# A Hymba-style decoder block: two plain tiles of the up-projection instead of three, with the activations' differences made beside their sums

## The chip, the cores and the metric
The kernel runs on one core of one Trainium2 chip. The metric is the device time of one launch in microseconds (us); lower is better. Engines are called TensorE, VectorE, ScalarE, GpSimd and SP (the queue that issues the transfers); in the profile they are PE (PEld is its weight load), DVE, ACT, POOL and SP.

## The reference, cut to what matters
One decoder block on 1024 tokens and 16 learned meta tokens, model width 1024. Two groups of attention heads read one projection; their outputs go through one output projection and are added to the residual. Then, and only this part is touched by the change:

```python
def _conv_ffn(xn, w_up, conv_w, conv_b, w_down):
    L = xn.shape[1]
    h = xn @ w_up
    hp = jnp.pad(h, ((0, 0), (CONV_WIDTH - 1, 0), (0, 0)))
    hc = conv_b + sum(conv_w[k] * hp[:, k:k + L] for k in range(CONV_WIDTH))
    gate, up = jnp.split(hc, 2, axis=-1)
    return (jax.nn.silu(gate) * up) @ w_down
```

`xn` is the normalised residual, 1024 wide, `w_up` is 1024 x 5632 and `w_down` 2816 x 1024, all in float32. A final norm follows.

## The kernel before, in words
**Precision.** Each float32 product is made of three matmuls on rounded numbers: every operand is split into a high part (ScalarE copies it to the matmul type) and a low part (the rest, by a subtraction), and high x high, high x low and low x high are summed in PSUM.

**The up-projection.** `w_up` is cut into 22 pairs of tiles of 128 columns (a gate tile and an up tile), called ff. The first `PLAIN` (3) pairs are multiplied plainly: a plain chunk (`plain_chunk`, L919) takes one pair and 256 tokens (plus 2 for the convolution), has 8 x 3 matmuls of 258 columns for the gate and as many for the up tile (48), then convolution, SiLU, product and a store to `gated`. `plain_chunk(..., h, s)` means half h of the sequence and quarter s in that half, so a pair has four chunks. The other 19 pairs go through the loop at L1105, which multiplies a 2 x 2 block form with seven products instead of eight (Strassen's scheme in Winograd's form): gate and up tile, the two halves of the model width and the two halves of the sequence are the blocks. A pass of it has 7 x 24 = 168 matmuls of 258 columns.

**What the loop needs.** Its activations are four blocks of the transposed input and four combinations: `s1`, `s2`, `s4` (made by `block_sums`, L970) and `s3` (made by `block_difference`, L984, written over a block of the input that only plain chunks of the second half still read). Both work on the rows of the normalised input, stored to DRAM earlier as `y_rows`, one block of 128 rows at a time (t = 4, 3, 2, 1, and t = 0 with two rows): `block_sums` loads the rows of both halves into tiles with the tags "ta" and "tb" (one buffer each), makes three combinations on VectorE (L978, L979, L980) in tiles `sa` (tag "wh") and `sb` (tag "wl"), and has TensorE transpose them (L180, four transposes of 128 x 128 for a half row); ScalarE and VectorE split the result (L183, L184). `block_difference` loads half rows into `rd` (tag "wl", L988, L989), subtracts in place (L990) and does the same. The tags "wh" and "wl" have two buffers each in the pool `pw`. The second plain pair's up tile has its parts in one buffer of each (`plain_weights`, L944, `last and i`), until its last chunk.

The loop's weights are prepared by `load_up` (L1035): gate and up tile are loaded raw, and four GpSimd subtractions (L1041 to L1044) make the combinations in tiles "ta" and "tb", the same buffers as the rows. `split_w` (L903) then splits each in 1.05 us of ScalarE (L907) and 2.4 us of GpSimd (L908). The order of a pass is: first product with the raw gate tile, second and third with `tb`, and so on.

**Order.** The kernel's text is an order of priority: a scheduler at compile time simulates the engines and fixes each engine's order of instructions; each engine then runs its instructions strictly in that order, waiting at semaphores. SP, too, issues transfers in its fixed order. A tile takes a free buffer of its tag when there is one, and waits for a release otherwise.

Around the change, the first two pairs' chunks of the second half stand before (L952 to L957). Then come the eight chunks, five sums and five differences of L1006 to L1024, and the loop.

Of the kernel before, what the change touches and what calls it, by code (L numbers as in the profile page):

```python
# [13 lines left out]
ALU = mybir.AluOpType  # L14
# [21 lines left out]

HALF = SEQ // 2
SUB = HALF // 2
PLAIN = 3
N_ROWS = 4  # L40
N_PAIRS = (NF - N_ROWS) // 2
G_PAIRS = 3
# [36 lines left out]
def q_span(t):  # L79

    return (0, 2) if t == 0 else (2 + P * (t - 1), P)
# [15 lines left out]
def hybrid_block(ctx: ExitStack, tc: tile.TileContext, x, meta, g_attn, w_in, lq1, lk1, lq2, lk2,  # L97
                 g_diff, g_sb, w_out, g_ffn, w_up, conv_w, conv_b, w_down, g_final, out):
    nc = tc.nc
# [6 lines left out]
    def bank(tag):  # L106
        return psum.tile([P, 512], F32, tag=tag, name=f"ps_{tag}", bufs=2)
# [39 lines left out]
    def rstd(pool, ss, n, tag):  # L147

        w = pool.tile([P, 4], F32, tag=tag, name=tag, bufs=4)
        l, y, m, u = (w[:n, i : i + 1] for i in range(4))  # L150
        nc.scalar.activation(l, ss, AF.Ln, bias=eps[:n], scale=1.0 / D)
        nc.scalar.activation(y, l, AF.Exp, scale=-0.5)
        nc.vector.tensor_scalar(m, ss, 1.0 / D, EPS, op0=ALU.mult, op1=ALU.add)
        nc.vector.tensor_scalar(u, m, y, y, op0=ALU.mult, op1=ALU.mult)
        nc.vector.tensor_scalar(u, u, -0.5, 1.5, op0=ALU.mult, op1=ALU.add)
        nc.vector.tensor_scalar(m, u, y, None, op0=ALU.mult)
        return m
# [17 lines left out]
    def transpose_half(src, n, places, tag):  # L175

        ps = bank(tag)
        v = ps.rearrange("p (a b) -> p a b", b=P)
        for j in range(4):
            nc.tensor.transpose(v[:, j, :n], src[:n, j * P : (j + 1) * P], ident[:n, :n])  # L180
        for hi, lo, c0, r0 in places:
            w = n - r0
            nc.scalar.copy(hi[:, :, c0 : c0 + w], v[:, :, r0:n])  # L183
            nc.vector.tensor_tensor(lo[:, :, c0 : c0 + w], v[:, :, r0:n], f(hi)[:, :, c0 : c0 + w], op=ALU.subtract)  # L184
# [269 lines left out]
    sums = {}  # L454
# [228 lines left out]
    def load_raw(src):  # L683
        raw = pw.tile([P, D], F32, tag="raw", name="raw", bufs=2)
        nc.sync.dma_start(raw, src)
        return raw
# [216 lines left out]
    def split_w(pool, tags, src, bufs):  # L903
        hi = pool.tile([P, D], F32R, tag=tags[0], name=tags[0], bufs=bufs)
        lo = pool.tile([P, D], F32R, tag=tags[1], name=tags[1], bufs=bufs)
        w = src.shape[-1]
        nc.scalar.copy(hi[:, :w], src)  # L907
        nc.gpsimd.tensor_tensor(lo[:, :w], src, f(hi)[:, :w], op=ALU.subtract)  # L908
        return hi, lo

    def conv(c, src, fc):

        n = c.shape[-1]
        taps = [src[:, j : j + n] if len(src.shape) == 2 else src[:, :, j : j + n] for j in range(3)]
        nc.scalar.activation(c, taps[2], AF.Identity, bias=cb[:, fc : fc + 1], scale=cw[:, fc, 2:3])
        for j in (1, 0):
            nc.vector.scalar_tensor_tensor(c, taps[j], cw[:, fc, j : j + 1], c, op0=ALU.mult, op1=ALU.add)

    def plain_chunk(ff, wts, h, s):  # L919
        cs = []  # L920
        for fc, (hi, lo), tag, ctag, bufs in ((ff, wts[0], "s", "o", 4), (NF + ff, wts[1], "av", "mc", 2)):
            ps = bank(tag)
            c0 = SUB * s
            for kt in range(KT):
                ks = slice(kt * P, (kt + 1) * P)
                for i, (a, b) in enumerate(((hi, yh[h]), (hi, yl[h]), (lo, yh[h]))):
                    nc.tensor.matmul(ps[:, : SUB + 2], a[:, ks], b[:, kt, c0 : c0 + SUB + 2],  # L927
                                     start=(kt == 0 and i == 0), stop=(kt == KT - 1 and i == 2))
            c = pn.tile([P, 342], F32, tag=ctag, name="c", bufs=bufs)[:, :SUB]
            conv(c, ps[:, : SUB + 2], fc)  # L930
            cs.append(c)
        cg, cu = cs
        nc.scalar.activation(cg, cg, AF.Silu)
        nc.vector.tensor_tensor(cg, cg, cu, op=ALU.mult)
        at = HALF * h + SUB * s
        nc.sync.dma_start(gated[ff, :, at : at + SUB], cg)
# [7 lines left out]
    def plain_weights(ff, last):  # L944
        ws = []
        for i in range(2):
            raw = load_raw(w_up[NF * i + ff])
            pool, tags, bufs = (pw, ("wh", "wl"), 2) if last and i else (pd, ("dh", "dl"), 3)
            ws.append(split_w(pool, tags, raw, bufs))
        return ff, ws  # L950
# [17 lines left out]
    HD = D // 2  # L968

    def block_sums(t):  # L970

        n, c = (P, q_span(t)[0]) if t else (2, 0)
        r0 = load_rows_of_y(y_rows[t, :n, :], n, "ta")
        r1 = load_rows_of_y(y_rows[t + NT // 2, P - n :, :], n, "tb")
        sa = pw.tile([P, D], F32, tag="wh", name="sa", bufs=2)[:n]
        sb = pw.tile([P, D], F32, tag="wl", name="sb", bufs=2)[:n]
        lo, hi = slice(0, HD), slice(HD, D)
        nc.vector.tensor_tensor(sa[:, lo], r1[:, lo], r1[:, hi], op=ALU.add)  # L978
        nc.vector.tensor_tensor(sa[:, hi], sa[:, lo], r0[:, lo], op=ALU.subtract)  # L979
        nc.vector.tensor_tensor(sb[:, hi], r0[:, hi], sa[:, hi], op=ALU.subtract)  # L980
        for (dst, src) in ((s1, sa[:, lo]), (s2, sa[:, hi]), (s4, sb[:, hi])):
            transpose_half(src, n, [(dst[0], dst[1], c, 0)], "tr")

    def block_difference(t):  # L984

        n, c = (P, q_span(t)[0]) if t else (2, 0)
        r = pw.tile([P, D], F32, tag="wl", name="rd", bufs=2)[:n]
        nc.sync.dma_start(r[:, :HD], y_rows[t, :n, :HD])  # L988
        nc.sync.dma_start(r[:, HD:], y_rows[t + NT // 2, P - n :, :HD])  # L989
        nc.vector.tensor_tensor(r[:, :HD], r[:, :HD], r[:, HD:], op=ALU.subtract)  # L990
        transpose_half(r[:, :HD], n, [(s3[0], s3[1], c, 0)], "tr")

    def load_rows_of_y(src, n, tag):
        rows = ps_.tile([P, D], F32, tag=tag, name="rows")[:n]
        nc.sync.dma_start(rows, src)
        return rows

    def sums(*ts_):
        for t in ts_:
            block_sums(t)  # L1000

    def differences(*ts_):
        for t in ts_:
            block_difference(t)

    first, second = plain  # L1006
    plain_chunk(*first, 0, 1)
    sums(4)
    plain_chunk(*first, 0, 0)
    sums(3)  # L1010
    third = plain_weights(2, False)
    plain_chunk(*third, 1, 1)
    sums(2)
    plain_chunk(*third, 1, 0)
    sums(1)
    plain_chunk(*second, 0, 1)
    sums(0)
    differences(4)
    plain_chunk(*second, 0, 0)
    differences(3)  # L1020
    plain_chunk(*third, 0, 1)
    differences(2, 1)
    plain_chunk(*third, 0, 0)
    differences(0)  # L1024
    banks.close()


# [18 lines left out]

    entries = [(ff, i) for ff in range(PLAIN, NF) for i in range(4)]
    ready = {}
# [55 lines left out]
    rest = sums_of = before = None  # L1104
    for ff in range(PLAIN, NF):  # L1105
        k = 4 * (ff - PLAIN)
        pool, tag, bufs = (pw, "wh", 2) if ff % 3 else (ps_, "cg", 1)
# [102 lines left out]
    for group in groups:  # L1210
        chains = {}
        n = len(group)
        for tag, begin, rows, cs in CHAINS:
# [3 lines left out]
            for t, j in order:  # L1217
                ps = chains[tag][t]
                hi, lo = taken[k + j]
# [12 lines left out]
    for t in range(1, NT + 1):  # L1232
# [11 lines left out]
        r = rstd(pn, ss, P, "rf")  # L1244
# [44 lines left out]
```

## Time and profile before

| what | value |
|---|---|
| median of 3 runs | 1430.29 us (1428.49 to 1432.56) |
| the profiled execution's own time | 1427.61 us |
| its span in the trace | 1425.9 us |
| granted clock of TensorE, mean | 0.985 |
| TensorE busy | 1347.5 us, 95% of the span |
| VectorE, ScalarE, GpSimd busy | 967.8, 714.9, 749.2 us |

The median is of whole runs on the device; the span is what the profiler recorded of one of them. A busy time is the union of an engine's instructions. A line such as L927 is a line of the kernel printed above. In a timeline, a row gives start, duration, engine, line, operation, what is written and read, and in brackets how long the engine had been idle and what released it.

### The profile page before, as it was taken

What the parts mean: (1) busy time and instruction counts of PE and PEld (TensorE: products, weight loads), DVE (VectorE), ACT (ScalarE), POOL (GpSimd) and SP (SyncE); (2) the same over time, 40 slices, a digit from 0 to 9 for tenths busy, and PEclk for the clock granted to TensorE, in tenths of its full rate; (3) what the DMA queues carried; (4) which work ended last, traced back from release to release, by engine and by line L of the source; (5) the groups of instructions that cost most, each with busy time, mean ns of one, the idle gap of its engine ahead of it and who ended that gap; (6) DMA issues with size and microseconds to landing.
All of it is one profiled execution on the core that took longest, in us unless ns stands there. A gap on an engine that the chain in (4) does not pass through costs nothing.

```text
span 1425.9 us, 24695 instructions
## 1 busy us (share of the span) xinstructions
PE 1347.5 (95%) x9000; PEld 1251.1 (88%) x9000; DVE 967.8 (68%) x1816; ACT 714.9 (50%) x1406; POOL 749.2 (53%) x769
## 2 busy tenths in 40 slices
PE   5999989999998998899999899999999996999997
PEld 5989989998987887678899899999999995888886
DVE  7377867778676787875877546555555565977755
ACT  6355655666575666542444344444454444534322
POOL 5145444235666676852103367766776573966620
PEclk9999999999999999999999999999999998999999
DMA  5154454221211127335633222323223325966502
GB/s 215 52 184 153 151 162 144 60 68 38 60 43 40 46 59 224 84 73 140 169 122 129 78 82 92 110 97 104 77 94 97 111 91 202 325 203 191 177 15 104
DMA packets 93569, 166.35 MB, mean 117 GB/s; under 512 B 11628, under 2 KB 46060, under 8 KB 93448
## 3 DMA queue, kind: packets, MB, share of 16 engines
q1 hardware_dynamic: 93448, 164.78, 37.0%
q8 instruction: 71, 1.16, 0.4%
q14 instruction: 50, 0.41, 0.1%
HBM read 111.49 MB, written 44.85 MB: 110 GB/s over the span
## 4 chain that ended last, share of the span: by engine, by line
PE 66%; DVE 9%; issue 4%; ACT 3%; POOL 2%; DMA 1%; SPq 0%; DVEq 0%; POOLq 0%; ACTq 0%
PE x L1063 27%; PE ps_x L1221 7%; PE ps_mm L297 7%; PE ps_y L1221 5%; PE ps_mm L745 5%; DVE s L501 3%; PE ps_av L588 2%; PE ps_tr L559 2%; PE ps_s L927 2%; PE ps_av L927 2%; PE ps_x L1239 2%; PE ps_y L1239 2%; PE ps_s L444 1%; PE ps_s L445 1%; PE ps_tr L180 1%
## 5 line engine op out<-in xcount | busy, mean ns | idle before, releaser
L297 PE MATMUL ps_mm<-xT_hi,wh 128*128 128x342 f32 (+7 forms) x552 | 182.6, 331 | 4.7 <-DVE qz L307 3.2
L297 PE MATMUL ps_mm<-xT_lo,wh 128*128 128x342 f32 (+7 forms) x552 | 180.1, 327 | 0.2 <-DVE xT_lo L184 0.2
L297 PE MATMUL ps_mm<-xT_hi,wl 128*128 128x342 f32 (+7 forms) x552 | 179.2, 326 | 0.0
L588 PE MATMUL ps_av<-aT,v 128*128 128x256 f32 (+3 forms) x608 | 130.8, 306 | 4.7 <-POOL aT L566 4.1
L908 POOL TENSOR_TENSOR dl<-raw,dh 128x1024 fp32r<-128x1024 f32 (+1 forms) x43 | 82.8, 1926 | 95.3 <-ACT dh L907 95.3
L1063 PE MATMUL x<-yh,dl 128*128 128x258 f32 x608 | 124.2, 286 | 0.0
L1063 PE MATMUL x<-yh,dh 128*128 128x258 f32 x608 | 123.7, 285 | 0.0
L1063 PE MATMUL x<-yl,dh 128*128 128x258 f32 x608 | 123.6, 285 | 0.0
L501 DVE TENSOR_TENSOR_SCAN s<-s 128x912 f32<-128x912 f32 (+6 forms) x72 | 100.3, 1396 | 21.8 <-POOL s L497 19.8
L1069 ACT COPY kept<-x 128x516 f32<-128x516 f32 x76 | 44.8, 590 | 135.2 <-PE x L1063 135.2
L297 PEld LDWEIGHTS ps_mm<-xT_hi,wh 128*128 128x128 f32 x552 | 105.5, 191 | 7.9 <-issue 2.4
L559 PE MATMUL ps_tr<-ident,a 128*128 128x128 f32 (+1 forms) x540 | 92.9, 277 | 18.8 <-DVE o L671 6.1
L1191 POOL TENSOR_TENSOR el<-down_raw,eh 128x512 fp32r<-128x512 f32 x53 | 91.3, 1753 | 35.9 <-ACT eh L1189 35.9
L588 PEld LDWEIGHTS ps_av<-aT,v 128*128 128x128 f32 (+2 forms) x608 | 95.2, 190 | 14.4 <-POOL aT L566 4.5
L297 PEld LDWEIGHTS ps_mm<-xT_lo,wh 128*128 128x128 f32 x552 | 105.6, 191 | 1.0 <-DVE xT_lo L184 0.5
L297 PEld LDWEIGHTS ps_mm<-xT_hi,wl 128*128 128x128 f32 x552 | 105.4, 191 | 0.3
L502 POOL TENSOR_TENSOR a<-a,s 128x912 f32<-128x912 f32 (+3 forms) x64 | 83.6, 1308 | 41.0 <-DVE s L501 33.6
L571 DVE TENSOR_TENSOR aT<-ps_tr,aT 128x512 fp32r<-128x512 f32 (+3 forms) x132 | 76.4, 585 | 34.2 <-ACT aT L570 33.4
L1063 PEld LDWEIGHTS x<-yh,dh 128*128 128x128 f32 x608 | 95.3, 191 | 0.0
L1063 PEld LDWEIGHTS x<-yl,dh 128*128 128x128 f32 x608 | 95.0, 191 | 0.0
L1063 PEld LDWEIGHTS x<-yh,dl 128*128 128x128 f32 x608 | 95.0, 191 | 0.0
L570 ACT CAST aT<-ps_tr 128x512 fp32r<-128x512 f32 (+3 forms) x132 | 66.6, 510 | 50.5 <-PE ps_tr L559 47.8
(306 smaller groups left out, 4057.5 us busy)
## 6 DMA issues: line engine op xcount, KB each, us to landing
raw<-in_w_up SPq DMA_DIRECT2D x44, 512.0 KB, 3.6
down_raw<-blocks SPq DMA_DIRECT2D x63, 256.0 KB, 3.8
raw<-in_w_in SPq DMA_DIRECT2D x24, 512.0 KB, 3.7
blocks<-cg SPq DMA_DIRECT2D x45, 256.0 KB, 3.5
raw<-in_w_down SPq DMA_DIRECT2D x18, 512.0 KB, 3.8
down_sums<-raw SPq DMA_DIRECT2D x18, 512.0 KB, 2.9
down_raw<-down_sums SPq DMA_DIRECT2D x36, 256.0 KB, 4.3
down_raw<-in_w_down SPq DMA_DIRECT2D x27, 256.0 KB, 4.1
```

The source lines that it names most:

```text
L297: nc.tensor.matmul(ps[:, :w], a[:, kt * P : (kt + 1) * P], b[:, kt, c0 : c0 + w], start=(kt == 0 and i == 0), stop=(kt == KT - 1 and i == 2))
L501: nc.vector.tensor_tensor_scan(s[:n, rev], s[:n, rev], s[:n, rev], 1.0, op0=ALU.mult, op1=ALU.bypass)
L502: (nc.gpsimd if t else nc.vector).tensor_tensor(b[:n, :keys], b[:n, :keys], s[:n, 1 : keys + 1], op=ALU.mult)
L559: pe_last[0] = nc.tensor.transpose(ps[:kn, at : at + qn], a[:qn, kk0 : kk0 + kn], ident[:qn, :qn])
L570: nc.scalar.copy(aT[:kn, 0, f0:end], ps[:kn, f0:end])
L571: nc.vector.tensor_tensor(aT[:kn, 1, f0:end], ps[:kn, f0:end], f(aT)[:kn, 0, f0:end], op=ALU.subtract)
L588: pe_last[0] = nc.tensor.matmul(av[:, :w], v[:kn, kt, vi, :], aT[:kn, ai, j * w : (j + 1) * w], start=job["count"] == 0, stop=job["count"] ...
L745: nc.tensor.matmul(ps[:n], a, b[:, hs], start=(j == 0 and i == 0), stop=(j == len(wo) - 1 and i == 2))
L908: nc.gpsimd.tensor_tensor(lo[:, :w], src, f(hi)[:, :w], op=ALU.subtract)
L1063: nc.tensor.matmul(x[:, s], w[a][:, ks], y[b][:, kt, SUB * s : SUB * s + SUB + 2], start=start and kt == 0 and i == 0, stop=kt == KT // 2 ...
L1191: engine.tensor_tensor(lo[:, cs], raw[:, cs], f(hi)[:, cs], op=ALU.subtract)
L1221: nc.tensor.matmul(ps, a[:, P * t : P * (t + 1)], b[:, upper], start=begin and j == 0 and i == 0, stop=j == n - 1 and i == 2, skip_group_c ...
```

## The change
The constant `PLAIN` goes from 3 to 2, so the third pair (ff = 2) becomes a pass of the loop, and its four plain chunks and weights go. The order of the sums and differences is rewritten: each block's difference now follows its sums, and the four chunks that are left stand between them. Two of the four row operations of a block (L980 in `block_sums`, L990 in `block_difference`) are issued on GpSimd instead of VectorE.

```diff
-PLAIN = 3
+PLAIN = 2
...
         nc.vector.tensor_tensor(sa[:, lo], r1[:, lo], r1[:, hi], op=ALU.add)
         nc.vector.tensor_tensor(sa[:, hi], sa[:, lo], r0[:, lo], op=ALU.subtract)
-        nc.vector.tensor_tensor(sb[:, hi], r0[:, hi], sa[:, hi], op=ALU.subtract)
+        nc.gpsimd.tensor_tensor(sb[:, hi], r0[:, hi], sa[:, hi], op=ALU.subtract)
...
-        nc.vector.tensor_tensor(r[:, :HD], r[:, :HD], r[:, HD:], op=ALU.subtract)
+        nc.gpsimd.tensor_tensor(r[:, :HD], r[:, :HD], r[:, HD:], op=ALU.subtract)
...
     first, second = plain
+    sums(4)
+    differences(4)
     plain_chunk(*first, 0, 1)
-    sums(4)
+    sums(3)
+    differences(3)
     plain_chunk(*first, 0, 0)
-    sums(3)
-    third = plain_weights(2, False)
-    plain_chunk(*third, 1, 1)
     sums(2)
-    plain_chunk(*third, 1, 0)
+    differences(2)
     sums(1)
+    differences(1)
     plain_chunk(*second, 0, 1)
     sums(0)
-    differences(4)
+    differences(0)
     plain_chunk(*second, 0, 0)
-    differences(3)
-    plain_chunk(*third, 0, 1)
-    differences(2, 1)
-    plain_chunk(*third, 0, 0)
-    differences(0)
     banks.close()
```

## Rows read from the trace of the kernel before

**Rows 1.** The page: span, and busy time of the engines.
```profile
span 1425.9 us, 24695 instructions
PE 1347.5 (95%) x9000; PEld 1251.1 (88%) x9000; DVE 967.8 (68%) x1816; ACT 714.9 (50%) x1406; POOL 749.2 (53%) x769
```

**Rows 2.** Busy time by stretch: its length, engines (instructions), clock, DMA share, GB/s.
```profile
739.30:799.00 59.70, 55.53 (x466) 54.72 (x464) 44.80 (x79) 26.41 (x49) 15.81 (x9) 1.00 0.44 141
799.00:819.50 20.50, 20.50 (x158) 20.48 (x158) 6.66 (x12) 6.01 (x10) 10.63 (x7) 0.92 0.10 34
819.50:1187.00 367.50, 367.50 (x3036) 367.50 (x3035) 205.63 (x286) 178.09 (x253) 240.01 (x139) 1.00 0.29 93
```

**Rows 3.** The chain of waits in order of time: start, length, what.
```profile
739.43 2.90 PE ps_s L927 x24
742.33 2.92 PE ps_av L927 x24
...
799.09 388.41 PE x L1063 x3192
```

**Rows 4.** Timeline of TensorE from 779 to 799 us.
```profile
779.51 0.40 PE L180 MATMUL ps_tr<-ident,sb 2*128 2x2 f32 x4
...
781.52 0.28 PE L927 MATMUL ps_av<-yh,wl 128*128 128x258 f32 x1
...
785.96 0.60 PE L180 MATMUL ps_tr<-ident,rd 128*128 128x128 f32 x4
...
794.85 0.29 PE L927 MATMUL ps_av<-yh,dl 128*128 128x258 f32 x1
798.72 0.38 PE L180 MATMUL ps_tr<-ident,rd 2*128 2x2 f32 x4 [3.58 <-DVE rd L990]
```

**Rows 5.** Timeline of SP's queue from 779 to 797 us.
```profile
779.94 0.32 SPq L988 DMA_DIRECT2D rd<-y_rows  x1
...
781.83 0.32 SPq L988 DMA_DIRECT2D rd<-y_rows  x1
...
786.59 0.32 SPq L988 DMA_DIRECT2D rd<-y_rows  x1
...
795.66 0.32 SPq L936 DMA_DIRECT2D gated<-c  x1
796.08 0.26 SPq L988 DMA_DIRECT2D rd<-y_rows  x1
```

**Rows 6.** Timeline of GpSimd from 750 to 800 us.
```profile
750.11 2.39 POOL L908 TENSOR_TENSOR dl<-raw,dh 128x1024 fp32r<-128x1024 f32 x1 [35.55 <-ACT dh L907]
...
775.17 1.30 POOL L1041 TENSOR_TENSOR ta<-raw 128x512 f32<-128x512 f32 x1 [1.41 <-DVE sb L980]
...
792.47 2.88 POOL L908 TENSOR_TENSOR dl<-tb,dh 128x1024 fp32r<-128x1024 f32 x1 [10.81 <-ACT dh L907]
```

**Rows 7.** Timeline of VectorE from 741 to 800 us.
```profile
741.20 0.69 DVE L978 TENSOR_TENSOR sa<-rows 128x512 f32<-128x512 f32 x1
...
750.88 2.18 DVE L980 TENSOR_TENSOR sb<-rows,sa 128x512 f32<-128x512 f32 x1
...
783.76 0.69 DVE L990 TENSOR_TENSOR rd<-rd 128x512 f32<-128x512 f32 x1 [0.84 <-DMA rd<-y_rows]
...
786.50 0.69 DVE L990 TENSOR_TENSOR rd<-rd 128x512 f32<-128x512 f32 x1 [1.19 <-DMA rd<-y_rows]
...
793.03 2.60 DVE L934 TENSOR_TENSOR c<-c 128x256 f32<-128x256 f32 x1
...
797.89 0.68 DVE L990 TENSOR_TENSOR rd<-rd 2x512 f32<-2x512 f32 x1 [0.74 <-DMA rd<-y_rows]
```

**Rows 8.** Transfers issued from 735 to 800 us: size, median us to landing.
```profile
rows<-y_rows SPq DMA_DIRECT2D x8, 512.0 KB, 4.2
```

**Rows 9.** Timeline of ScalarE: the cast of the loop's second weights.
```profile
791.34 1.05 ACT L907 CAST dh<-tb 128x1024 fp32r<-128x1024 f32 x1 [1.36 <-PE ps_s L927]
```

**Rows 10.** Groups by line, 739.3 to 799 us: busy us, mean ns, idle before.
```profile
L917 DVE SCALAR_TENSOR_TENSOR c<-ps_s,cw,c 128x256 f32<-128x256 f32 x16 | 7.7, 478 | 3.1 <-ACT c L915 2.9
...
L934 DVE TENSOR_TENSOR c<-c 128x256 f32<-128x256 f32 x8 | 6.6, 828 | 0.1
```

## The prediction before the run
> **What bounds the kernel now.** I began with the page: TensorE is busy for nearly the whole span [rows 1], so what matters is where it is not, or where it does work that could be shorter. The table of stretches shows two neighbouring stages [rows 2]. From 739.3 to 799.0 us (call it the transition) TensorE is busy for 55.53 of 59.7 us while it computes eight chunks of plain tiles and transposes the sums of the activations; from 799 to 1187 us the up-projection loop keeps it busy without a gap. The loop is therefore priced by its matmuls alone: 367.5 us for 3,036 of them is 0.121 us each, and the 168 of one pass of the loop take 20.34 us. A chunk's 48 matmuls take 2.90 + 2.92 = 5.82 us in the chain of waits [rows 3]. The other engines have slack in the transition (VectorE 44.8, ScalarE 26.4, GpSimd 15.8 us), so only waits in order can hurt there.
>
> Then TensorE's timeline at the seam: after the last plain matmul it waits 3.58 us for the last difference [rows 4], and the loop's first matmul stands at 799.02. Its granted clock is 0.92 in the next 20.5 us against 1.00 later [rows 2]; 158 matmuls there should take 19.1 us, so the restart cost some 1.4 us.
>
> **Removed from TensorE, added to it.** One tile leaves the plain form: four chunks vanish between 739.3 and 799 (the third tile's whole work stands there), 4 x 5.82 = 23.3 us. One pass of the loop comes, 20.34 us. If TensorE's work alone set the end, the transition would end at 795.14 (end of the last plain matmul) less 23.3, less 0.6 of idle time inside, plus 0.4 for the last transposes: 771.6. Let X be the time at which the loop effectively starts; the change is then X + 20.34 - 799.02, that is X - 778.7. TensorE's work alone gives 771.6 - 778.7 = -7.1 us. The question is whether the sums and differences, which lose half of their cover, still fit.
>
> **The chain of one buffer.** They do not run freely. The tag "wl" has two buffers; while the second tile's weights live, its low part holds one, and the sums' `sb` and the differences' `rd` share the other. The trace shows this sharing: the load of the first `rd` is issued at 779.94, right behind the last transposes of `sb` (779.51 + 0.40), the second at 781.83, when the last matmul on the second tile's low weights has ended, the third at 786.59, behind the transposes of the first `rd` (785.96 + 0.60) [rows 4, 5]. Before, all five sums ran first and the differences followed, mostly after that tile was done. Now each difference stands between two sums, so one block of rows costs, on this one buffer:
> - L980 on GpSimd. GpSimd's 512-column subtraction takes 1.30 us [rows 6], VectorE's 0.69 [rows 7].
> - Transposes of `sb`: 0.15 us after their input, as at 798.72, and 0.60 long [rows 4, 7]: 0.75.
> - The load of `rd`: 3.82 us from issue to the subtraction in the first case, 4.67 in the second [rows 5, 7]; I take the mean, 4.25.
> - L990 on GpSimd, 1.30, and transposes again, 0.75.
>
> The sum is 8.35 us a block. Other bounds are wider: by the row of 785.96 the transposes stood 1.5 us behind their input at 784.45, since TensorE's order is fixed; with 1 us more at both places a block costs 10.3. Nothing in the chain can be much below 7.9 (the shorter load).
>
> The first `sb` can start at 742.6: L978 starts at 741.20 [rows 7], unchanged because what precedes it is, and two VectorE steps of 0.69 follow. L980 of the four whole blocks then starts at 742.6, 751.0, 759.3 and 767.7. The rows of the next block are loaded beside this (4.2 us [rows 8]) and are no limit. Meanwhile TensorE, always with plain matmuls to do, ends the second tile at 739.43 + 23.3 + 13 groups of transposes at 0.45 (55.53 less eight chunks, over 20 groups) = 768.6. From then on there are two buffers, and the next difference loads at 768.7 without waiting.
>
> **The tail of the transition.** L980 of the last whole block ends at 769.0. The two-row block's load takes 1.81 us (796.08 to 797.89 [rows 5, 7]), L979 0.69, L980 1.30: 772.8. Only now is the buffer "ta" free for the loop's weights, which need it in both kernels. GpSimd's queue then holds L990 of the last whole block (772.95 to 774.3), L1041 (775.6), L990 of the two-row block (776.9), L1043 (778.2); ScalarE's cast of `tb` takes 1.05 [rows 9] and L908 2.4 [rows 6]: the loop's second weights are ready at 781.7. The first product, on raw weights, runs on TensorE before that; the second waits for the low part from its fifth matmul on and ends 20 x 0.121 later, at 784.1. Two products are 48 x 0.121 = 5.8, so **X is 778.3**, and the change is 778.3 - 778.7 = -0.4 us. The restart at a lower granted clock, 1.4 us, was paid before and is paid again; its bounds are none of it and twice it.
>
> If GpSimd makes the loop's weights before the two L990, X is 775.7 (-3.0). If every transposition waits 1 us more, the second tile's end still opens the other buffer at 768.7, the last whole L980 waits for its rows instead (763.2 + 1.3 + 4.2 + 0.69 = 769.4), and with one collision of 1.3 us X is 781.3 (+2.6). So the forecast's own range is -3.0 to +2.6.
>
> **The smaller edits.** GpSimd loses the third tile's two splits (4.8 us) and gets ten subtractions (13 us) and one pass of the loop, where it is busy 240 us in 18 passes, 13 in each: covered by TensorE's 20.34, so nothing; uncovered it would be those 13. SP's queue runs in order and carries four stores of `gated` fewer; a store that waits holds loads behind it, as at 795.66, where `rd` was issued 2.4 us late because L934 had taken 2.60 us [rows 5, 7]. Each of the four left can still do so: nothing to 2.4 us, and I take nothing, since two buffers leave room at the end. What is stored of the third tile is now stored by the loop, long before its use.
>
> **Rivals.**
> *TensorE stays the bound.* Loads at their short end (3 x 0.43 us earlier) and the loop's weights ahead of the L990: X is 774.4 or less, with 771.6 as the floor; -4.3 to -7.1, middle **1424.6**; with the restart saved too, 1421.8. For it: no large idle time but the last in the transition before [rows 4]. Against it: it needs every order to fall well. Chance 0.24.
>
> *The second buffer comes too late.* TensorE runs in order. If the transposes are queued ahead of plain matmuls and their rows are late, the plain matmuls wait behind them, the second tile ends only with the chain, and the single buffer serves all blocks: with p us a block, L980 of the two-row block starts at 742.6 + 4p, the second weights are ready 8.6 us later (four subtractions, L980 first, then 1.05 and 2.4), and the change is 4p - 30.9. That is slower beyond the noise from p = 8.8 on; at p = 9.6, **1437.8**. For it: the measured 1.5 us. Against it: before, TensorE hardly waited inside the transition. Chance 0.18.
>
> *VectorE and GpSimd exclude each other.* L980 took 2.18 us and L934 2.60 where GpSimd's L908 was running (750.11 to 752.50, 792.47 to 795.35), each ending some 0.3 to 0.6 us after it [rows 6, 7]. VectorE loses half its convolutions and products (7.7 + 3.3: half of twice the convolution row and half of the product row [rows 10]), and ten subtractions (6.9): 26.9 us remain. If each of the 14 left with two inputs in SBUF waits out a whole GpSimd subtraction, 18.2 us come on top; 739.3 + 45.1 = 784.4, +5.7, **1436.0**. It decides only if nearly all of them collide. Chance 0.08. The Trainium skill (SBUF — State Buffer, "Who interferes with whom") says of these pairs that whichever issues first has the shared ports for the whole instruction and the other is blocked fully; that rule speaks against splitting such sums over the two engines, and the trace agrees at the two places named. By it alone, moving work to GpSimd frees no VectorE time that two SBUF inputs need.
>
> That the change does not do what it says can be set aside: the loop's range starts at `PLAIN`, so the tile moves whole.
>
> **Numbers.** The profiled execution took 1427.61 us; the runs' median is 1430.29, 0.2% above. The differences are added to the median: 1429.9. About 0.3% (4.3 us) is what a measurement tells from no change. Same 0.50 (the forecast), faster 0.24, slower 0.18 + 0.08 = 0.26. The range reaches to near the middle of the slower rival and below the faster one's: 1422.5 to 1438.
>
> **What would show it.** In the changed profile: L1063 starts its dense run at 776 to 782; L980 on GpSimd comes every 8 to 9 us three times, with each `rd` load issued right behind transposes; TensorE is busy until about 768 and then idles for some 10 us with single products between; the loop's second entry waits for L908 on `tb`. Wrong, if plain matmuls wait behind transposes before 765, if the loads of `rd` are issued without regard to `sb`, or if the dense run starts before 774 or after 783.

## The result and the profile after

The changed kernel takes 1441.76 us (median of 4 runs, 1440.50 to 1442.55) against 1429.59 us before in the same comparison: a ratio of 1.0082 with a 95% interval of 1.0068 to 1.0095. It is slower, by some 10 to 14 us.

The page of the changed kernel, to be read beside [rows 1]:

```profile
span 1440.8 us, 24658 instructions
PE 1352.0 (94%) x8976; PEld 1253.2 (87%) x8976; DVE 961.4 (67%) x1800; ACT 716.9 (50%) x1406; POOL 771.0 (54%) x785
```

The span is 14.9 us longer. Not all of it belongs to the change: up to the transition the engines' orders of instructions are the same in both kernels, yet the last weight load of the output projection (L745) starts at 711.0 us in the profile before and at 716.8 after, and in the 14 profiles of this study it lies anywhere between 710.6 and 716.8; the changed kernel's is the latest. So from here on two profiles are compared by what comes behind that landmark. Its row in both kernels (first and last start, us; before, then after):

```profile
L745 PEld LDWEIGHTS ps_mm<-wh,mt x128: 186/188/337, 546.0 to 711.0; 128*128 128x128 f32 x128
```
```profile
L745 PEld LDWEIGHTS ps_mm<-wh,mt x128: 186/188/337, 551.0 to 716.8; 128*128 128x128 f32 x128
```

The loop of the changed kernel (L1059, which is L1063 of before) in the chain of waits, to be read beside the last of [rows 3]:

```profile
791.79 409.79 PE x L1059 x3360
```

From the landmark to the loop's end it was 476.5 us before (799.09 + 388.41 - 711.0) and is 484.8 now (791.79 + 409.79 - 716.8): +8.3. The loop starts 13.1 us earlier and lasts 21.4 us longer. The pass that was added accounts for 20.3 of these, so 1 us more is lost inside the loop; another 0.8 us lies behind it (span less the loop's end).

This measure hides 1.5 us. Between the landmark and the first pair's chunk (0, 1) TensorE does the same work in both kernels, with one wait of 1.98 us in each, but it took 28.27 us at a mean granted clock of 0.94 before and 26.72 us at 1.00 in the changed kernel (columns as in [rows 2]; before, then after):

```profile
711.00:739.27 28.27, 26.30 (x208) 25.73 (x207) 19.55 (x46) 13.83 (x27) 2.41 (x1) 0.94 0.33 118
```
```profile
716.80:743.52 26.72, 24.74 (x207) 24.31 (x206) 19.47 (x46) 13.76 (x27) 2.38 (x1) 1.00 0.36 124
```

Why the clock differed there is not shown; the orders are the same. From the chunk's first matmul to the loop's end it is 448.2 us before and 458.1 now: +9.8. With the 0.8 behind the loop that is 10.6 us, inside the 10 to 14 of the runs.

Busy time by stretch in the changed kernel, columns as in [rows 2]: the plain chunks, the gap behind them, the loop's first 20.5 us, the rest of the loop.

```profile
743.50:769.90 26.40, 26.36 (x222) 26.14 (x220) 17.23 (x33) 10.31 (x20) 6.48 (x4) 1.00 0.51 157
769.90:791.70 21.80, 10.19 (x52) 8.06 (x52) 10.84 (x19) 7.52 (x15) 13.80 (x11) 0.58 0.36 106
791.70:812.20 20.50, 20.50 (x149) 20.48 (x150) 3.42 (x6) 6.61 (x10) 12.95 (x9) 0.86 0.17 52
812.20:1201.60 389.40, 389.36 (x3214) 389.14 (x3213) 216.23 (x303) 188.47 (x267) 253.99 (x148) 1.00 0.28 92
```

TensorE does its four chunks without a gap, and then has 21.8 us in which 52 transposes are all it gets. Its granted clock falls to 0.58 there and is still 0.86 in the loop's first 20.5 us (0.92 before).

GpSimd's timeline in the changed kernel, from the first sums to the loop's weights:

```profile
747.55 1.28 POOL L980 TENSOR_TENSOR sb<-rows,sa 128x512 f32<-128x512 f32 x1 [27.30 <-DVE sa L979]
...
758.38 1.51 POOL L990 TENSOR_TENSOR rd<-rd 128x512 f32<-128x512 f32 x1 [0.85 <-DMA rd<-y_rows]
762.07 1.29 POOL L980 TENSOR_TENSOR sb<-rows,sa 128x512 f32<-128x512 f32 x1 [2.19 <-PE ps_tr L180]
771.11 1.26 POOL L990 TENSOR_TENSOR rd<-rd 128x512 f32<-128x512 f32 x1 [7.75 <-DVE c L917]
772.33 1.27 POOL L980 TENSOR_TENSOR sb<-rows,sa 128x512 f32<-128x512 f32 x1
778.16 1.26 POOL L990 TENSOR_TENSOR rd<-rd 128x512 f32<-128x512 f32 x1 [4.55 <-DMA rd<-y_rows]
780.21 1.49 POOL L980 TENSOR_TENSOR sb<-rows,sa 128x512 f32<-128x512 f32 x1 [0.79 <-DVE sa L979]
...
784.24 1.75 POOL L990 TENSOR_TENSOR rd<-rd 128x512 f32<-128x512 f32 x1 [1.29 <-DMA rd<-y_rows]
785.96 1.25 POOL L980 TENSOR_TENSOR sb<-rows,sa 2x512 f32<-2x512 f32 x1
...
789.90 1.25 POOL L990 TENSOR_TENSOR rd<-rd 2x512 f32<-2x512 f32 x1
791.12 1.28 POOL L1040 TENSOR_TENSOR ta<-raw,tb 128x512 f32<-128x512 f32 x1
792.37 2.37 POOL L908 TENSOR_TENSOR dl<-tb,dh 128x1024 fp32r<-128x1024 f32 x1
```

The sums and differences take turns: L980 starts at 747.55, 762.07, 772.33, 780.21 and 785.96, that is 14.5, 10.3, 7.9 and 5.8 us apart, 9.6 in the mean. In the first distance they wait for each other on the shared buffer. The second tile's last plain matmul ends at 769.85, and from then on there are two buffers: the second distance ends behind L990 in GpSimd's queue, the third on a reload of the rows, for which VectorE's sum (L979) waits, and the last on such a reload and then behind L990 again. The sum before the fourth L980:

```profile
779.28 0.69 DVE L979 TENSOR_TENSOR sa<-sa,rows 128x512 f32<-128x512 f32 x1 [0.82 <-DMA rows<-y_rows]
```

TensorE's side of it, and the loads of `rd` on SP's queue:

```profile
752.83 0.60 PE L180 MATMUL ps_tr<-ident,sb 128*128 128x128 f32 x4
...
766.27 0.60 PE L180 MATMUL ps_tr<-ident,sb 128*128 128x128 f32 x4
...
769.57 0.28 PE L927 MATMUL ps_av<-yh,wl 128*128 128x258 f32 x1
772.43 0.66 PE L180 MATMUL ps_tr<-ident,rd 128*128 128x128 f32 x4 [2.57 <-POOL rd L990]
...
776.05 1.06 PE L180 MATMUL ps_tr<-ident,sb 128*128 128x128 f32 x4
779.47 1.11 PE L180 MATMUL ps_tr<-ident,rd 128*128 128x128 f32 x4 [2.36 <-POOL rd L990]
...
791.21 0.58 PE L180 MATMUL ps_tr<-ident,rd 2*128 2x2 f32 x4 [1.63 <-POOL rd L990]
791.72 0.58 PE L1059 MATMUL x<-yh,dh 128*128 128x258 f32 x1
```
```profile
753.46 0.32 SPq L988 DMA_DIRECT2D rd<-y_rows  x1
...
766.90 0.32 SPq L988 DMA_DIRECT2D rd<-y_rows  x1
...
773.15 0.32 SPq L988 DMA_DIRECT2D rd<-y_rows  x1
...
780.67 0.32 SPq L988 DMA_DIRECT2D rd<-y_rows  x1
```

Each `rd` load stands right behind transposes, the first two behind those of `sb` (752.83 + 0.60, 766.27 + 0.60), the third behind those of the `rd` before (772.43 + 0.66). The transposes that take 0.60 us while TensorE is busy take up to 1.1 in the gap.

### The profile page after: what moved, and what is told of

It is laid out like the page before. It is cut to its first block, busy times and chain, and to the rows that moved or that the text cites. A ratio compares the mean times of both kernels' runs of the same rounds, so it can differ in the third digit from the quotient of the medians.

```text
span 1440.8 us, 24658 instructions
## 1 busy us (share of the span) xinstructions
PE 1352.0 (94%) x8976; PEld 1253.2 (87%) x8976; DVE 961.4 (67%) x1800; ACT 716.9 (50%) x1406; POOL 771.0 (54%) x785
## 4 chain that ended last, share of the span: by engine, by line
PE 49%; DMA 1%; DVE 1%; POOL 1%; ACT 0%; issue 0%; SPq 0%; DVEq 0%; POOLq 0%; ACTq 0%
PE x L1059 28%; PE ps_x L1217 7%; PE ps_y L1217 5%; PE ps_x L1235 2%; PE ps_y L1235 2%; PE ps_mm L745 1%; PE ps_s L927 1%; PE ps_av L927 1%; PE ps_tr L180 1%; DMA rd<-y_rows 1%; PE ps_mm L722 0%; POOL rd L990 0%; DMA down_raw<-in_w_down 0%; DVE yn L894 0%; DMA blocks<-cg 0%
## 5 line engine op out<-in xcount | busy, mean ns | idle before, releaser
L1059 PE MATMUL x<-yh,dl 128*128 128x258 f32 x640 | 130.9, 286 | 0.0
L1059 PE MATMUL x<-yh,dh 128*128 128x258 f32 x640 | 130.8, 286 | 0.0
L1059 PE MATMUL x<-yl,dh 128*128 128x258 f32 x640 | 130.4, 285 | 0.0
L908 POOL TENSOR_TENSOR dl<-raw,dh 128x1024 fp32r<-128x1024 f32 (+1 forms) x43 | 81.0, 1886 | 69.4 <-ACT dh L907 69.4
L1059 PEld LDWEIGHTS x<-yh,dh 128*128 128x128 f32 x640 | 100.8, 192 | 0.0
L1059 PEld LDWEIGHTS x<-yl,dh 128*128 128x128 f32 x640 | 100.5, 192 | 0.0
L1059 PEld LDWEIGHTS x<-yh,dl 128*128 128x128 f32 x640 | 100.2, 192 | 0.0
```

Of the source, the lines that this page charges most:

```text
L1059: nc.tensor.matmul(x[:, s], w[a][:, ks], y[b][:, kt, SUB * s : SUB * s + SUB + 2], start=start and kt == 0 and i == 0, stop=kt == KT // 2 ...
```

## The experiments

Three measures are quoted. The first expectations use the transition, from the first matmul of the first pair's chunk (0, 1) to the loop's first matmul: 59.75 us before, 48.20 changed. It misleads where the work ahead of that chunk changes too (the runs with two sets of rows). The second goes from the landmark to the loop's end. The third, from the chunk's first matmul to the loop's end, leaves out the 1.5 us of clock named above; in the runs with two sets of rows it misleads as the transition does. Each of these is read from one profiled execution, and how far they vary between executions of one kernel was not measured, so no conclusion rests on a difference of about 1 us between two of them. All runs of a comparison share runs of the kernel before.

| run | transition | landmark to loop's end | chunk to loop's end | median us (before) | ratio, 95% interval |
|---|---|---|---|---|---|
| before | 59.75 | 476.5 | 448.2 | 1429.6 | |
| changed | 48.20 | 484.8 | 458.1 | 1441.8 | 1.0082 (1.0068 to 1.0095) |
| e1_vector | 46.39 | 482.3 | 455.6 | 1436.0 (1429.2) | 1.0052 (1.0033 to 1.0071) |
| e2_own_rd | 39.89 | 476.8 | 448.6 | 1429.9 (1429.2) | 1.0017 (1.0000 to 1.0034) |
| e3_sums_first | 47.86 | 485.9 | 457.6 | 1438.1 (1429.2) | 1.0063 (1.0039 to 1.0087) |
| e4_three_gpsimd | 61.29 | 478.8 | 450.6 | 1431.7 (1429.2) | 1.0015 (1.0001 to 1.0030) |
| e5_own_rd_vector | 41.86 | 479.2 | 451.0 | 1433.2 (1428.5) | 1.0034 (1.0023 to 1.0046) |
| e6_two_row_sets | 36.94 | 477.1 | 445.8 | 1429.6 (1428.5) | 1.0007 (0.9998 to 1.0016) |
| e7_row_sets_vector | 40.45 | 480.1 | 449.3 | 1428.9 (1428.5) | 1.0008 (0.9996 to 1.0019) |
| e8_three_own_rd | 65.71 | 482.7 | 454.5 | 1435.8 (1428.5) | 1.0049 (1.0034 to 1.0064) |
| e9_own_rd_banks | | 476.1 | 448.0 | 1427.6 (1428.4) | 0.9995 (0.9986 to 1.0004) |
| e10_row_sets_banks | | 476.7 | 445.5 | 1429.2 (1428.4) | 1.0002 (0.9989 to 1.0014) |
| e11_banks_only | | 485.9 | 457.7 | 1438.2 (1428.4) | 1.0067 (1.0049 to 1.0085) |
| e12_small_block_early | 34.33 | 469.9 | 441.6 | 1423.7 (1428.7) | 0.9962 (0.9948 to 0.9975) |

**e1_vector**: the change without its move to GpSimd.

```diff
-        nc.gpsimd.tensor_tensor(sb[:, hi], r0[:, hi], sa[:, hi], op=ALU.subtract)
+        nc.vector.tensor_tensor(sb[:, hi], r0[:, hi], sa[:, hi], op=ALU.subtract)
...
-        nc.gpsimd.tensor_tensor(r[:, :HD], r[:, :HD], r[:, HD:], op=ALU.subtract)
+        nc.vector.tensor_tensor(r[:, :HD], r[:, :HD], r[:, HD:], op=ALU.subtract)
```

> Two plain tiles and the new order, but both subtractions (L980, L990) back on VectorE. Measure: the transition, from the first matmul of the first pair's chunk (0, 1) to the loop's first matmul: 59.75 us before, 48.2 us changed; break-even with the longer loop is 39.4. Theory A (sums and differences take turns on one buffer, and that chain is the end): five L980 and five L990 get 0.6 us shorter, but they queue with VectorE's convolutions; 2 to 4 us less than changed, transition 44 to 46, 1437 to 1440 us. Theory B (the move to GpSimd is the cost: slower instructions, exclusion with VectorE, L980 behind L990 in one queue): 8 us or more less, transition 40 or under, 1434 or less.

Transition 46.39, just above theory A's range, and 2.5 us less than changed by the landmark, as by the chunk; the median, 1436.0, lies 1 us under the range. That is theory A's size and not theory B's: by the traces the move to GpSimd costs 2.5 us in this order, and most of the loss stays.

**e2_own_rd**: the change with one tile in a buffer of its own.

```diff
-        r = pw.tile([P, D], F32, tag="wl", name="rd", bufs=2)[:n]
+        r = ps_.tile([P, D], F32, tag="cg", name="rd", bufs=1)[:n]
```

> The changed kernel with one edit: rd gets a buffer of its own (tag cg, which is free until the loop's second pass). Theory A: a difference no longer holds the sums' buffer; L980 then comes every 6 to 7 us (rows reload 4.2, two steps of VectorE, L980), and the transition falls to 38 to 42 us: 1431 to 1435. Theory B (GpSimd is the cost): 3 us less at most, transition 45 to 48. Theory D (with four chunks gone the cover is too short whatever the buffers): transition 44 or more.

Transition 39.89, and 8.0 us less than changed by the landmark (9.4 of the 9.8 by the chunk); the ratio falls from 1.0082 to 1.0017. GpSimd's timeline of this run:

```profile
743.41 1.30 POOL L990 TENSOR_TENSOR rd<-rd 128x512 f32<-128x512 f32 x1 [28.25 <-DVE sa L979]
744.67 1.28 POOL L980 TENSOR_TENSOR sb<-rows,sa 128x512 f32<-128x512 f32 x1
750.26 1.29 POOL L980 TENSOR_TENSOR sb<-rows,sa 128x512 f32<-128x512 f32 x1 [4.31 <-DVE sa L979]
...
759.22 1.29 POOL L980 TENSOR_TENSOR sb<-rows,sa 128x512 f32<-128x512 f32 x1 [0.81 <-DVE sa L979]
...
768.85 1.51 POOL L980 TENSOR_TENSOR sb<-rows,sa 128x512 f32<-128x512 f32 x1 [0.78 <-PE ps_tr L180]
...
773.95 1.27 POOL L980 TENSOR_TENSOR sb<-rows,sa 2x512 f32<-2x512 f32 x1
```

The first difference is made even before the first `sb`, and L980 comes every 7.3 us in the mean instead of 9.6 (6 to 7 were expected). The median, 1429.9, is 1 us under theory A's range. The shared buffer is what makes the change lose: one edit to it takes nearly all of the loss away. The edit also lets the scheduler order the engines differently, as the first row shows, so what it removes is the shared buffer together with the order that follows from it.

**e3_sums_first**: two plain tiles in the order of before.

```diff
     first, second = plain
-    sums(4)
-    differences(4)
     plain_chunk(*first, 0, 1)
-    sums(3)
-    differences(3)
+    sums(4)
     plain_chunk(*first, 0, 0)
+    sums(3)
     sums(2)
-    differences(2)
     sums(1)
-    differences(1)
     plain_chunk(*second, 0, 1)
     sums(0)
-    differences(0)
+    differences(4)
     plain_chunk(*second, 0, 0)
+    differences(3)
+    differences(2, 1)
+    differences(0)
```

> Two plain tiles, GpSimd as in the change, but the order of before with the third pair's lines taken out: all sums, then the differences. Theory A: the sums run at 6 to 8 us a block and end some 35 us in, five differences follow in twos at 6.3 us: transition 46 to 52, 1440 to 1445, no better than the change. Theory C (the new order is the cost): transition 40 or under, 1433 or less.

The transition is within theory A's range; the median, 1438.1, is 2 us under it. By the landmark it is 1.1 us worse than changed, by the chunk 0.4 better, by the medians 3.6 better with overlapping ratios: no difference is shown. The new order is not what costs: with four chunks of cover fewer, either order leaves the work uncovered as long as the buffers are those.

**e4_three_gpsimd**: the kernel before with both subtractions on GpSimd (the two lines of e1_vector the other way round).

> The kernel before (three plain tiles, sums first) with only the two subtractions moved to GpSimd. Theory A: eight chunks cover the chain; transition 58 to 61, within 2 us of before. Theory B: 4 us or more slower than before.

Transition 61.29, 2.3 us more than before by the landmark, 1.0015 by the runs: between the two theories' figures, nearer A's, and the same size as in e1_vector.

**e5_own_rd_vector**: e2_own_rd and e1_vector together.

> Own buffer for rd (as in the run with that edit alone: transition 39.9 us) and L980, L990 back on VectorE. Theory A (the chain of buffers): each step in the chain 0.6 us shorter, five blocks, as between the change and its VectorE twin (1.8): transition 37 to 39, 1427 to 1430. Theory B (GpSimd and its exclusion with VectorE are half of the cost once the buffer is free): transition 35 or under.

Neither. By the traces it is 2.4 us slower than e2_own_rd, but the runs' intervals overlap (from 1.0023 to 1.0034). So with `rd` in its own buffer GpSimd looks like the better place for the two subtractions, by as much as it was the worse one before; the runs don't settle it. L980 of the last whole block starts 59.2 us behind the landmark here and 57.2 in e2_own_rd. That VectorE's queue of convolutions and products holds it up is argued from the timeline, not isolated.

**e6_two_row_sets** and **e7_row_sets_vector**: e2_own_rd with the rows of two blocks in other buffers; e7 with VectorE as well.

```diff
-        r0 = load_rows_of_y(y_rows[t, :n, :], n, "ta")
-        r1 = load_rows_of_y(y_rows[t + NT // 2, P - n :, :], n, "tb")
+        r0 = load_rows_of_y(y_rows[t, :n, :], n, "raw" if t in (4, 2) else "ta")
+        r1 = load_rows_of_y(y_rows[t + NT // 2, P - n :, :], n, "raw" if t in (4, 2) else "tb")
```

> Own buffer for rd, GpSimd as in the change, and the rows of blocks 4 and 2 in the two raw buffers, so that the next block's rows load while this one's are used. If the reload of the rows (4.2 us behind each L980) is the next link of the chain: L980 every 5 to 6 us, transition 35 to 37, 1424 to 1427. If TensorE's fixed order or the engines are the next link: within 1 us of 39.9.

> Own buffer for rd, two sets of rows, and both subtractions on VectorE. Theory A: the three links together, transition 33 to 36 against TensorE's own 31.9, 1422 to 1426. If the loop's weights, made from tiles ta and tb after the last sums, are the next link: 36 to 38.

477.1 and 480.1 against 476.8 and 479.2 without the second set: no gain. The shorter transitions (36.94, 40.45) are paid ahead of the chunk at which the measure starts: from the landmark to that chunk e6 takes 31.3 us where e2_own_rd takes 28.2. With other buffers for the first block's rows its L980 runs at 723.56 already, its sums stand in VectorE's queue ahead of work on the last normalised rows, and TensorE waits 3.69 us for that instead of 1.98, with a mean clock of 0.89 instead of 0.94. The other four L980 still come 8.6 to 9.3 us apart (749.67, 758.25, 767.57, 776.18), not the 5 to 6 expected, so the reload of the rows is not what sets their pace. In the runs' medians e6 and e7 don't differ; by the landmark VectorE is again 3 us worse.

**e8_three_own_rd**: the kernel before with `rd` as in e2_own_rd.

> The kernel before with one edit: rd in a buffer of its own. Theory A (before, too, the differences end the transition by the shared buffer): the 3.6 us wait at the seam goes with its 1.4 us restart, transition 55 to 57, 3 to 5 us less than before. If the wait at the seam comes from SP's order (a gated store holding the load): within 1 us of before.

A miss: 6.2 us slower than before. With three plain tiles the differences stand at the end, when the second tile's weights have gone, and there the shared tag gave them two buffers [rows 5]; one of their own makes them wait for each other. The trace shows it: loads of `rd` are issued at 784.06, 791.39, 796.95 and 802.39, the last three each within 0.1 us behind the transposes of the difference before (790.77 + 0.60, 796.29 + 0.63, 801.27 + 1.09). A buffer helps by how many the tile gets at its time, not by being its own.

**e9_own_rd_banks**, **e10_row_sets_banks**, **e11_banks_only**: half of the transposes in the two PSUM banks of tag "mm", on top of e2_own_rd, of e6_two_row_sets and of the change alone.

```diff
-        for (dst, src) in ((s1, sa[:, lo]), (s2, sa[:, hi]), (s4, sb[:, hi])):
-            transpose_half(src, n, [(dst[0], dst[1], c, 0)], "tr")
+        for (dst, src, tag) in ((s1, sa[:, lo], "tr"), (s2, sa[:, hi], "mm"), (s4, sb[:, hi], "tr")):
+            transpose_half(src, n, [(dst[0], dst[1], c, 0)], tag)
...
-        transpose_half(r[:, :HD], n, [(s3[0], s3[1], c, 0)], "tr")
+        transpose_half(r[:, :HD], n, [(s3[0], s3[1], c, 0)], "mm")
```

> Own buffer for rd, GpSimd as in the change, and two of a block's four groups of transposes go to the two PSUM banks of tag mm, idle here, instead of all four through the two of tag tr. Measure from here on: last matmul on the output projection's weights (L745) to the end of the loop: 476.5 us before, 484.8 changed, 476.8 with the own buffer alone. Theory E (the banks' turn, transpose, copy, subtraction, is the next link: in the own-buffer run transposes stand up to 6 us behind their input): 3 to 6 us less, 471 to 474, 1423 to 1427. Theory F (the reload of rows and the load of rd are the link): within 1 us of 476.8.

> The same with two sets of rows too (blocks 4 and 2 in the raw buffers). Two sets without the banks gave 477.1, no better than without. If banks and rows are links of one chain and each hides the other: 469 to 472, 1421 to 1425, TensorE nearly the bound. If only the banks count: as the run with own buffer and banks.

> The changed kernel with the four banks alone; rd still shares the sums' buffer. Theory A (the shared buffer ties sums and differences to turns; transposes wait on it): 2 to 5 us less than changed, 480 to 483, 1436 to 1440, for the first sb no longer waits 4 us for its transposes. Theory E alone (the banks were the whole cause): 476 or less, 1430 or less.

e11 is no better than the change in the traces (485.9 against 484.8, and 457.7 against 458.1 by the chunk), so four banks alone don't shorten it there, and theory A's 2 to 5 us less are a miss; the median, 1438.2, is in theory A's range, with a ratio that overlaps the change's. The first `sb` does wait less for its transposes, 2.35 us (744.04 to 746.39) instead of 4.0, but the next L990 then stands behind a split of weights (L908) in GpSimd's queue, and the first distance of two L980 is 14.4 us as before (742.75 to 757.13). e9 gains 0.7 us on e2_own_rd, e10 0.4 on e6: not theory E's 3 to 6, and less than these measures can tell from nothing. But e9's TensorE shows where the time now sits, in one wait for the last difference, and GpSimd's timeline shows why that is late:

```profile
770.11 0.66 PE L180 MATMUL ps_mm<-ident,rd 128*128 128x128 f32 x4 [0.36 <-POOL rd L990]
...
771.33 0.40 PE L180 MATMUL ps_tr<-ident,sb 2*128 2x2 f32 x4 [0.23 <-POOL sb L980]
776.85 0.58 PE L180 MATMUL ps_mm<-ident,rd 2*128 2x2 f32 x4 [5.12 <-POOL rd L990]
```
```profile
771.35 1.30 POOL L1037 TENSOR_TENSOR ta<-raw 128x512 f32<-128x512 f32 x1
772.73 1.50 POOL L1039 TENSOR_TENSOR tb<-raw,ta 128x512 f32<-128x512 f32 x1
774.30 1.27 POOL L1040 TENSOR_TENSOR ta<-raw,tb 128x512 f32<-128x512 f32 x1
775.54 1.26 POOL L990 TENSOR_TENSOR rd<-rd 2x512 f32<-2x512 f32 x1
```

TensorE waits 5.12 us for a subtraction of two rows that stands in GpSimd's queue behind three combinations of the loop's weights.

**e12_small_block_early**: e9_own_rd_banks with the two-row block third and the last whole block's difference on VectorE.

```diff
-        nc.gpsimd.tensor_tensor(r[:, :HD], r[:, :HD], r[:, HD:], op=ALU.subtract)
+        (nc.vector if t == 1 else nc.gpsimd).tensor_tensor(r[:, :HD], r[:, :HD], r[:, HD:], op=ALU.subtract)
...
     sums(3)
     differences(3)
+    sums(0)
+    differences(0)
     plain_chunk(*first, 0, 0)
     sums(2)
     differences(2)
+    plain_chunk(*second, 0, 1)
     sums(1)
     differences(1)
-    plain_chunk(*second, 0, 1)
-    sums(0)
-    differences(0)
     plain_chunk(*second, 0, 0)
```

> Own buffer for rd, four banks, and the tail shortened: the two-row block stands third instead of last, and the last block's difference alone is on VectorE, so that it no longer waits in GpSimd's queue behind the loop's weights (5.1 us of TensorE's idle time in the run with buffer and banks). If that queue is the last link: from the last L745 matmul to the loop's end 470 to 472 us against 476.2 before, 1422 to 1425, 0.3 to 0.5% less than before. If a whole block at the end (4.2 us of reload instead of 1.8) takes it back: 475 to 478, no change.

469.9 us, 6.6 less than before (476.5, not the 476.2 of the expectation), and 1423.7 us by the runs: 0.9962 (0.9948 to 0.9975), that is 4 to 7 us less. This version beats both kernels. Which of its two edits to e9 does it was not separated. Its stretches (transition, then the loop's first 20.4 us), end of the transition on TensorE, and loop:

```profile
739.25:773.60 34.35, 32.82 (x275) 31.61 (x273) 27.67 (x50) 15.56 (x32) 18.35 (x13) 1.00 0.54 183
773.60:794.00 20.40, 20.40 (x172) 20.40 (x170) 8.06 (x12) 9.96 (x14) 16.38 (x11) 1.00 0.20 61
```
```profile
771.75 0.28 PE L927 MATMUL ps_av<-yh,wl 128*128 128x258 f32 x1
773.19 0.63 PE L180 MATMUL ps_mm<-ident,rd 128*128 128x128 f32 x4 [1.16 <-DVE rd L990]
```
```profile
773.82 407.06 PE x L1059 x3360
```

TensorE idles 1.5 of 34.35 us, the clock stays at 1.00, and the loop takes 407.06 us where its matmuls alone need 3,360 x 0.12105 = 406.7 (367.5 / 3,036 = 0.12105 us each); in the changed kernel it took 409.79. That is what the change's arithmetic on TensorE is worth when little is left uncovered.

## Why the prediction was wrong

**TensorE's account was right.** Four chunks went, 20.3 us of loop came, and e12_small_block_early, where TensorE is nearly the bound again, gains 6.6 us in the trace and 4 to 7 by the runs. The forecast had worked out 7.1 with the restart paid, and 1421.8, that is 8.5 less, with it saved; e12 saves 1.6 of it (the loop loses 0.4 us instead of 2.0), so some 2 us of the floor are not reached.

**"The sum is 8.35 us a block" is the step that failed.** That the two tiles take turns on one buffer was right: e2_own_rd takes 8.0 of the 8.3 us away with that buffer alone. The size of a turn was wrong, by the term "Transposes of `sb`: 0.15 us after their input". That figure came from the idle end of the kernel before. While TensorE still had plain matmuls queued ahead, the transposes in the changed kernel stood 4.0 us behind (L980 ends at 748.83, transposes at 752.83), 1.45 (759.89 to 761.34) and, for the second `sb`, 2.9 (763.36 to 766.27); TensorE had no idle time in front of them, so it was its fixed order that held them. The first load of `rd` took 4.92 us to its subtraction instead of 4.25. The first turn so lasts 14.5 us where 8.35 was forecast; the upper bound of 10.3, with 1 us at each place, was itself too low. The trace of the kernel before had this: there all five `sb` waited 4.4 to 6.1 us for their transposes, the second from the end of L980 in [rows 7] (750.88 + 2.18 = 753.06) to

```profile
758.55 0.60 PE L180 MATMUL ps_tr<-ident,sb 128*128 128x128 f32 x4
```

**"From then on there are two buffers" brought little.** The second tile's last plain matmul ends at 769.85, 26.3 us behind the chunks' start, earlier than the 29.2 forecast. But L980 of the third whole block, whose inputs were there, stood in GpSimd's queue behind L990 of the block before, and that waited for the second half of its load (issued at 767.27) until 771.11: L980 started at 772.33. (The bracket of that row names L917 on VectorE, of whose output L990 reads nothing.) The forecast had treated the two subtractions as if each could start when its own buffer was free; on GpSimd they share one order.

**The tail** was forecast at 8.9 us from the last L980 to the loop's second weights (772.8 to 781.7) and took 7.5 (787.21 to 794.74).

**Added up.** Counted from the chunks' first matmul (739.27 and 743.52), the loop's second weights were forecast at 42.4 us and came at 51.2. Of these 8.8 us the first L980 is 0.7, the first turn 6.2, the second 1.9, the third -0.5, the last distance 2.0 (5.8 instead of 3.8: its L979 waited for rows, and its L980 stood behind L990) and the tail -1.4, which is 8.9 with the forecast's roundings. With 1.0 us more of restart that is 9.8 of the 10.2 us between the forecast's -0.4 and the +9.8 measured from chunk to loop's end.

**The restart** was not simply paid again: behind a gap of 21.8 us at clock 0.58 the loop loses 3.1 us (409.79 less 406.7), before it was 2.0 (388.41 less 3,192 x 0.12105).

**The rivals.** "The second buffer comes too late" set 9.6 us a block and 1437.8 us; the mean distance of L980 is 9.6, and the time 1441.8. That its size came near is luck, for its cause was not there: plain matmuls didn't wait behind transposes (26.36 of 26.40 us busy), the transposes waited behind plain matmuls, and the second tile was done early. It had a chance of 0.18, and the range ended 0.2 us above its middle. "TensorE stays the bound" is nearly what e12_small_block_early does, with four edits to the changed kernel (buffer, banks, order, one subtraction on VectorE). "VectorE and GpSimd exclude each other" is seen but not decisive: in the changed kernel the ten subtractions on GpSimd take 1.0 us longer in all than at 1.26 us each, and one of VectorE's sums beside them 0.6 longer (1.31 us for 0.69), far from the 18.2 of that rival. For one, L990 at 784.24 takes 1.75 us instead of 1.26 beside a VectorE sum that began 0.06 us before it:

```profile
784.18 0.68 DVE L979 TENSOR_TENSOR sa<-sa,rows 2x512 f32<-2x512 f32 x1 [1.39 <-DMA rows<-y_rows]
```

The Trainium skill (SBUF — State Buffer, "Who interferes with whom") lets whichever of such a pair issues first hold the ports to its end; the row agrees, with 0.5 us lost. In the traces the sign of the move to GpSimd turned with the buffers: 2.5 us lost in the change, 2.4 gained in e2_own_rd, which no price of a single instruction foretells. The runs leave the second open.

## What to carry to other kernels

When work that covers a chain is taken away, price the chain with its waits in the engines' fixed orders, not with the best latency seen: a step that shares a queue with long work starts late, however early its input is. Two tiles that take turns on one buffer are a serial chain even when their data are independent; look for a tag that is idle at that time, and count how many buffers each has then. Put the shortest piece of a serial chain early, and let no last piece stand behind the next stage's work in a queue (here the two were done together).

## What the runs showed of the hardware

TensorE's granted clock in the changed kernel was 0.58 in a gap in which it did 10.2 us of transposes in 21.8 us; a group of four took 1.06 to 1.12 us there against 0.60 at clock 1.00, so most of the gap ran at the lower of its two levels, 1.2 GHz. The sparse transposes thus became slower just where the chain waited for them: of the nine groups of 128 rows in the gap the first two took 0.66 and 0.60 us and the other seven so much, and 7 x 0.5, up to 3.5 us, is an estimate of what that cost, some of it beside other waits. In e12_small_block_early, with 1.5 us idle in 34.35, the clock stayed at 1.00, and the loop ran 2.7 us faster than behind the gap.
